# Two unused tiles in the constants pool that move x and xT from 128 to 0 modulo 512 bytes in SBUF

## The chip, the cores and the metric

The kernel runs on one core of one Trainium2 chip. The metric is the device time of one execution in microseconds (us), the median of several runs. The profile comes from one further execution.

## What is computed

One encoder block with float32 weights on 256 tokens of width 1024: a half-step SwiGLU feed-forward, a mixer with two parallel branches, and a second half-step feed-forward. Cut to what matters for the work on the matrix engine:

```python
def block(x):                                     # x: (256, 1024), F = 4096
    h = rmsnorm(x, ffn1_pre_g)
    x = x + 0.5 * rmsnorm((silu(h @ w_gate) * (h @ w_up)) @ w_down, ffn1_post_g)
    h = rmsnorm(x, mix_pre_g)
    q, k, v, f, u, sv, ga, gb = split(h @ w_in)
    o_a = forgetting_attention(q, k, v, f)        # 8 heads of 128, causal, with a decay from f
    o_b = gelu(u) * (w_s @ layernorm(gelu(sv)) + b_s)
    m = sigmoid(ga) * o_a + sigmoid(gb) * o_b
    x = x + rmsnorm(m @ w_out, mix_post_g)
    h = rmsnorm(x, ffn2_pre_g)
    return x + 0.5 * rmsnorm((silu(h @ w_gate2) * (h @ w_up2)) @ w_down2, ffn2_post_g)
```

## The kernel before

**Precision.** Each float32 operand of a large product is split into a high part (rounded to fp32r, the matrix engine's fast float32) and a low part (the remainder): ScalarE casts the high part (L83), VectorE subtracts (L84). A product is three matmuls: high by high, high by low and low by high.

**Tiling.** The normalised activations are transposed on TensorE and kept in `xT` as [128 rows of the width, 8 blocks k, 2 token tiles t, high or low, 128 tokens] (L69, written by `to_xT`, L156 to L162). "Tokens stationary" means that in most products the 128 tokens are the stationary operand, which a weight load (LDWEIGHTS) brings into the array, and 512 columns of a weight matrix are the moving operand. `proj` (L212 to L218) does this for gate, up, v, sv, u, ga, gb and the output projection: for each k it runs `xT[high]` by `hi`, `xT[high]` by `lo`, `xT[low]` by `hi`, so two matmuls of three move `hi` and one `lo`. Every matmul has a weight load of its own, also where two in a row use the same stationary operand.

**Other stationary operands.** The down projection (`down`, L340 to L351) has `hT` as stationary operand, the hidden activations, with the same three terms. Three of the four up blocks of each feed-forward use `fast` (L270 to L329), a Strassen-Winograd scheme with 7 products of 12 matmuls each instead of 8: three of them take their stationary operand from `xT` (tiles `A` twice and `D` once), four from `parts`, sums and differences of quarters of x (tiles `B`, `C` and, the first time, `D`). All of these go through the one matmul call at L285 with the same order of terms.

**Moving xT.** In `attention` (L481) the roles are reversed: `wide` (L191 to L197) has the weights stationary and moves all 512 columns of `xT[:, k]` for the high weights, and the 256 high columns for the low weights. The forget gates (L455) move `xT` as well.

**Memory.** SBUF addresses are given as bytes within a partition; they follow from the order in which the pools and their tiles are made, in steps of 32 bytes. The constants pool comes first, with `x` (L66), `xT` (L69), `ident` (L71), `power` (L72), `idle` (L646) and the small tiles of the mixer. Then come five buffers `raw` of 8192 bytes for loaded weights, four each of `hi` and `lo`, two gains, ten intermediate tiles of 2048 bytes, three buffers of 8192 bytes for `hT` and the mixer's tiles, and `parts`. All rows of `xT`, `hT` and `parts` that one matmul loads are 512 bytes long, and they follow one another at steps of 512 bytes, so each has the same address modulo 512 as its tile.

**Order.** The order on each engine follows from the program and from priorities at build time; all loads go through one queue (SP). The weight buffers are filled some blocks ahead of the products that use them.

Of the kernel before, what the change touches and what calls it, by code (L numbers as in the profile page):

```python
# [15 lines left out]
F32 = mybir.dt.float32  # L16
# [6 lines left out]
P = 128  # L23
# [22 lines left out]
def block(ctx: ExitStack, tc: tile.TileContext, a: dict, out: bass.AP):  # L46
    nc = tc.nc
    const = ctx.enter_context(tc.tile_pool(name="const", bufs=1))
# [14 lines left out]
        return mid.tile(shape, F32, tag="m", name=name)  # L63


    x = const.tile([P, NT, D], F32, name="x")  # L66
    for t in range(NT):
        nc.sync.dma_start(out=x[:, t, :], in_=a["x"][t])
# [1 line left out]

    ident = const.tile([P, P], F32, name="ident")  # L71
    power = const.tile([P, 4], F32, name="power")  # L72
    nc.vector.memset(power, -0.5)

    def gain(name, by=D):
# [689 lines left out]
```

## Time and profile before

| | |
|---|---|
| median of 3 runs | 770.52 us (769.61 to 773.78) |
| profiled execution: its own time | 769.38 us |
| profiled execution: span from first to last instruction | 767.6 us |
| granted TensorE clock, mean over the span | 0.999 |
| TensorE busy, matmuls | 746.9 us, 3446 instructions |
| VectorE busy | 539.0 us, 516 instructions |
| ScalarE busy | 381.0 us, 376 instructions |
| moved by DMA | 141.61 MB, 184 GB/s over the span |

TensorE is read from the chain of work that ended last and from the timeline: a matmul's own recorded duration includes its way through the pipeline, which overlaps with the next matmul, so what it costs is the distance from its start to the next start. In the chain, a run of matmuls is one piece, whose length divided by its count is that distance.

### The profile page before, as it was taken

The numbers are of one execution on the slowest core, as the hardware profiler recorded it, in microseconds if no ns is written. First come the engines' busy times: TensorE is split into PE (matmuls) and PEld (weight loads), VectorE is DVE, ScalarE is ACT, GpSimd is POOL, SyncE is SP. The second block draws the span as 40 slices with busy tenths as digits, with TensorE's granted clock in tenths as the row PEclk, the third lists the DMA queues.
The fourth block names the chain that finished last, engine by engine and source line by source line (L and its number), as shares of the span: only waits on it lengthen the run. The fifth ranks groups of instructions, "written<-read, shape, count | busy, mean of one in ns | idle before, by whom it ended". The sixth has DMA issues, their size and how long they took to land. (4 is left out here: it accounts for less than half of the span.)

```text
span 767.6 us, 8470 instructions
## 1 busy us (share of the span) xinstructions
PE 746.9 (97%) x3446; PEld 608.1 (79%) x3446; DVE 539.0 (70%) x516; ACT 381.0 (50%) x376; POOL 21.5 (3%) x32
## 2 busy tenths in 40 slices
PE   5999999999999999999999999889999999999996
PEld 2888888888888877888888888678888888888885
DVE  6584798589479875746486547858479958947982
ACT  5553465446445474754544435645346545644541
POOL 1000000000000021000020000300000000000000
PEclk9999999999999999999999999999999999999999
DMA  9785158418515835643427435437515741851521
GB/s 338 286 311 191 61 211 293 153 68 338 197 55 213 330 136 184 257 161 110 158 117 275 164 111 219 163 118 266 178 70 198 301 159 59 334 210 55 199 75 56
DMA packets 21974, 141.61 MB, mean 184 GB/s; under 512 B 3184, under 2 KB 3440, under 8 KB 5680
## 3 DMA queue, kind: packets, MB, share of 16 engines
q1 hardware_dynamic: 21936, 141.08, 50.0%
q8 instruction: 27, 0.44, 0.2%
q14 instruction: 11, 0.09, 0.0%
HBM read 140.02 MB, written 1.05 MB: 184 GB/s over the span
## 5 line engine op out<-in xcount | busy, mean ns | idle before, releaser
L217 PE MATMUL g<-hi_g,xT 128*128 128x512 f32 x512 | 166.7, 396 | 0.3 <-ACT hi_g L83 0.2
L350 PE MATMUL y<-hi_d,hT 128*128 128x512 f32 x512 | 148.0, 393 | 0.0
L217 PEld LDWEIGHTS g<-hi_g,xT 128*128 128x128 f32 x512 | 96.4, 188 | 23.1 <-ACT hi_g L83 1.0
L350 PEld LDWEIGHTS y<-hi_d,hT 128*128 128x128 f32 x512 | 95.7, 188 | 20.1
L84 DVE TENSOR_TENSOR lo_g<-raw_g,hi_g 128x2048 fp32r<-128x2048 f32 (+1 forms) x33 | 73.4, 2225 | 44.9 <-ACT hi_g L83 44.9
L217 PE MATMUL g<-lo_g,xT 128*128 128x512 f32 x256 | 101.3, 396 | 2.8 <-DVE lo_g L84 2.7
L84 DVE TENSOR_TENSOR lo_d<-raw_d,hi_d 128x2048 fp32r<-128x2048 f32 x32 | 73.0, 2287 | 39.4 <-ACT hi_d L83 39.4
L350 PE MATMUL y<-lo_d,hT 128*128 128x512 f32 x256 | 81.1, 393 | 0.0
L83 ACT CAST hi_g<-raw_g 128x2048 fp32r<-128x2048 f32 (+1 forms) x33 | 61.2, 1856 | 34.7 <-PE u L217 10.5
L83 ACT CAST hi_d<-raw_d 128x2048 fp32r<-128x2048 f32 x32 | 60.8, 1915 | 26.9 <-PE g L217 8.8
L217 PE MATMUL u<-hi_u,xT 128*128 128x512 f32 x192 | 61.7, 396 | 0.0
L217 PEld LDWEIGHTS g<-lo_g,xT 128*128 128x128 f32 x256 | 48.3, 189 | 14.7 <-DVE lo_g L84 3.8
L350 PEld LDWEIGHTS y<-lo_d,hT 128*128 128x128 f32 x256 | 47.9, 188 | 9.9
L289 DVE TENSOR_TENSOR raw_u<-raw_u,raw_u 128x2048 f32<-128x2048 f32 x24 | 55.0, 2292 | 0.8
L356 ACT ACTIVATE sg<-g 128x512 f32<-128x512 f32 x32 | 18.9, 598 | 67.3 <-PE g L217 67.3
L196 PE MATMUL qk<-xT,hi_qk 128*128 128x512 f32 x128 | 46.3, 400 | 0.0
L83 ACT CAST hi_u_3p<-raw_u 128x2048 fp32r<-128x2048 f32 x14 | 26.6, 1915 | 32.9 <-DVE raw_u L289 25.1
L217 PEld LDWEIGHTS u<-hi_u,xT 128*128 128x128 f32 x192 | 36.1, 188 | 8.3
L84 DVE TENSOR_TENSOR lo_u<-raw_u,hi_u 128x2048 fp32r<-128x2048 f32 x12 | 27.4, 2289 | 16.6 <-ACT hi_u L83 16.5
L84 DVE TENSOR_TENSOR lo_u_3p<-raw_u,hi_u_3p 128x2048 fp32r<-128x2048 f32 x14 | 31.9, 2288 | 9.6 <-ACT hi_u_3p L83 9.6
L217 PE MATMUL u<-lo_u,xT 128*128 128x512 f32 x96 | 37.9, 394 | 0.0
L83 ACT CAST hi_u_1p<-raw_u 128x2048 fp32r<-128x2048 f32 x14 | 26.8, 1914 | 20.3 <-DVE raw_u L289 9.5
(254 smaller groups left out, 1273.2 us busy)
## 6 DMA issues: line engine op xcount, KB each, us to landing
raw_u<-in_u SPq DMA_DIRECT2D x32, 1024.0 KB, 4.8
raw_d<-in_dn SPq DMA_DIRECT2D x32, 1024.0 KB, 4.7
raw_g<-in_g SPq DMA_DIRECT2D x31, 1024.0 KB, 4.9
raw_qk<-in_w_qk SPq DMA_DIRECT2D x8, 1024.0 KB, 5.1
raw_v<-in_w_v SPq DMA_DIRECT2D x4, 1024.0 KB, 5.4
raw_sv<-in_w_sv SPq DMA_DIRECT2D x4, 1024.0 KB, 4.7
raw_u<-in_w_u SPq DMA_DIRECT2D x4, 1024.0 KB, 4.7
raw_ga<-in_w_ga SPq DMA_DIRECT2D x4, 1024.0 KB, 4.7
```

What stands on the lines that cost most here:

```text
L83: return [nc.scalar.copy(out=hi, in_=src), nc.vector.tensor_tensor(out=lo, in0=src, in1=hi.bitcast(F32), op=ALU.subtract)]
L84: nc.vector.tensor_tensor(out=lo, in0=src, in1=hi.bitcast(F32), op=ALU.subtract)]
L196: nc.tensor.matmul(ps, lhsT=hi, rhs=xT[:, k], start=k == 0, stop=False, skip_group_check=True)
L217: nc.tensor.matmul(ps, lhsT=xT[:, kh * 4 + k, t, xs, :], rhs=v, start=kh == 0 and k == 0 and q == 0, stop=kh == 1 and k == 3 and q == 2)
L289: nc.vector.tensor_tensor(out=out, in0=p, in1=q, op=ALU.add)
L350: nc.tensor.matmul(ys[t][c], lhsT=hTs[f // 4][:, f % 4, t, xs, :], rhs=w[:, c * 512:(c + 1) * 512], start=f == 0 and q == 0, stop=f == NF ...
L356: nc.scalar.activation(out=sg, in_=y, func=AF.Silu)
```

## The change

```diff
@@ -63,6 +63,7 @@
         return mid.tile(shape, F32, tag="m", name=name)
 
 
+    const.tile([P, 96], F32, name="pad0")
     x = const.tile([P, NT, D], F32, name="x")
     for t in range(NT):
         nc.sync.dma_start(out=x[:, t, :], in_=a["x"][t])
@@ -70,6 +71,7 @@
 
     ident = const.tile([P, P], F32, name="ident")
     power = const.tile([P, 4], F32, name="power")
+    const.tile([P, 32], F32, name="pad1")
     nc.vector.memset(power, -0.5)
 
     def gain(name, by=D):
```

The two tiles are never written or read. `pad0` takes 384 bytes of each partition, `pad1` 128. The instructions on every engine, their order, their waits, the buffers that each tile gets and the places in PSUM are the same before and after; only addresses in SBUF differ:

| tile | before | modulo 512 | after | modulo 512 |
|---|---|---|---|---|
| `x` | 16512 | 128 | 16896 | 0 |
| `xT` | 24704 | 128 | 25088 | 0 |
| `ident` | 41088 | 128 | 41472 | 0 |
| `power` | 41600 | 128 | 41984 | 0 |
| `idle` | 41632 | 160 | 42144 | 160 |
| `raw`, first buffer | 44288 | 256 | 44800 | 256 |
| `hi`, first buffer | 85248 | 256 | 85760 | 256 |
| `lo`, first buffer | 118016 | 256 | 118528 | 256 |
| `hT`, first buffer | 179456 | 256 | 179968 | 256 |
| `parts` | 204032 | 256 | 204544 | 256 |

Everything from `idle` on moves up by 512 bytes, and so keeps its address modulo 512.

## Rows read from the trace of the kernel before

**Rows 1.** The page: busy time of each engine, granted clock in 40 slices.
```profile
PE 746.9 (97%) x3446; PEld 608.1 (79%) x3446; DVE 539.0 (70%) x516; ACT 381.0 (50%) x376; POOL 21.5 (3%) x32
...
PEclk9999999999999999999999999999999999999999
```

**Rows 2.** Groups by form: line, engine, operation, shapes, count | busy us, mean ns | idle.
```profile
L217 PE MATMUL g<-hi_g,xT 128*128 128x512 f32 x512 | 166.7, 396 | 0.3 <-ACT hi_g L83 0.2
L350 PE MATMUL y<-hi_d,hT 128*128 128x512 f32 x512 | 148.0, 393 | 0.0
...
L217 PEld LDWEIGHTS g<-hi_g,xT 128*128 128x128 f32 x512 | 96.4, 188 | 23.1 <-ACT hi_g L83 1.0
L350 PEld LDWEIGHTS y<-hi_d,hT 128*128 128x128 f32 x512 | 95.7, 188 | 20.1
...
L217 PE MATMUL u<-hi_u,xT 128*128 128x512 f32 x192 | 61.7, 396 | 0.0
...
L217 PE MATMUL v<-hi_v,xT 128*128 128x512 f32 x64 | 20.6, 396 | 0.0
...
L285 PE MATMUL u_1A<-hi_u_1p,xT 128*128 128x512 f32 x32 | 10.7, 395 | 0.0
```

**Rows 3.** The chain that ended last: start us, length us, engine, tile, line, count.
```profile
502.43 16.73 PE g L217 x72
519.16 13.93 PE u L217 x60
...
576.48 2.80 PE u_1A L285 x12
579.28 2.75 PE u_1C L285 x12
582.03 2.72 PE y L350 x12
584.75 2.73 PE u_1B L285 x12
...
738.66 22.74 PE y L350 x100
```

**Rows 4.** Timeline of TensorE in a gate block: start us, length us, what, count.
```profile
505.51 0.64 PE L217 MATMUL g<-hi_g,xT 128*128 128x512 f32 x2
505.99 0.39 PE L217 MATMUL g<-lo_g,xT 128*128 128x512 f32 x1
```

**Rows 5.** Timeline, matmul and the weight load beside it.
```profile
587.31 0.40 PE L285 MATMUL u_1A<-hi_u_1p,xT 128*128 128x512 f32 x1
587.31 0.19 PEld L285 LDWEIGHTS u_1A<-lo_u_1p,xT 128*128 128x128 f32 x1
```

**Rows 6.** Timeline of TensorE in the query and key products, every sixth matmul.
```profile
312.75 0.28 PE L197 MATMUL qk<-xT,lo_qk 128*128 128x256 f32 x1
...
313.80 0.28 PE L197 MATMUL qk<-xT,lo_qk 128*128 128x256 f32 x1
...
314.85 0.28 PE L197 MATMUL qk<-xT,lo_qk 128*128 128x256 f32 x1
```

**Rows 7.** Groups by form: other operations on moved and unmoved tiles.
```profile
L84 DVE TENSOR_TENSOR hT<-hp,hT 128x512 fp32r<-128x512 f32 x32 | 21.4, 684 | 0.0
...
L371 PE MATMUL hp<-ident,sg 128*128 128x128 f32 x128 | 18.5, 272 | 0.0
...
L84 DVE TENSOR_TENSOR xT<-tp_f,xT 128x512 fp32r<-128x512 f32 x8 | 5.2, 684 | 0.0
...
L594 PE MATMUL mx<-vn,ws 128*128 128x128 f32 x32 | 4.2, 274 | 0.0
```

**Rows 8.** DMA issues: what, queue, count, KB each, median us to landing.
```profile
x<-in_x SPq DMA_DIRECT2D x2, 512.0 KB, 3.4
...
out<-x SPq DMA_DIRECT2D x4, 256.0 KB, 2.0
```

## The prediction

> **What bounds the kernel now.** I read three views in this order. First the busy times: the matmuls occupy TensorE for 746.9 of 767.6 us, VectorE is at 70% and ScalarE at 50% [rows 1]. Only 20.7 us of the span lie outside matmuls, so nearly everything the change can do must show as the distance from one matmul to the next, and nothing on another engine can be worth much unless TensorE comes to wait for it. [...]
>
> Second the chain of waits, which gives that distance. With `xT` as stationary operand it is (16.73 + 13.93) / (72 + 60) = 232.3 ns in the gate and up products; with `hT` it is 22.74 / 100 = 227.4 ns in the last long run of the down projection [rows 3]. Third, a control inside one piece of code: the Strassen products of line 285 have the same moving tiles, the same order of terms and the same 12 matmuls, and lie a few us apart. With `xT` stationary (`u_1A`) they take 2.80 / 12 = 233.3 ns each, with `parts` stationary 2.75 / 12 = 229.2 (`u_1C`) and 2.73 / 12 = 227.5 (`u_1B`); a short block with `hT` in between takes 2.72 / 12 = 226.7 [rows 3]. So 5 ns per matmul go with the tile `xT`, not with the line, the loop or the stage.
>
> Where in the matmul the 5 ns lie is not seen directly. The weight loads are recorded with 188 ns for `xT` and for `hT` alike, and the matmuls with 396 against 393 ns [rows 2]. The load for the next matmul begins together with the current one, both at 587.31 us [rows 5], so two reads of SBUF, one of 512 bytes per partition and one of 2048, run side by side in every interval. What sets `xT` apart from `hT`, `parts`, `hi` and `lo` is its address: it begins at 128 modulo 512, all the others at 256, so it alone is not at a multiple of 256. It also lies lowest of all, and the trace before cannot separate the one from the other.
>
> [...]
>
> **The change part by part.** *Instructions.* None is added, removed or moved, and no wait, queue or buffer changes. The padding is never touched. This part costs nothing, and no cover is needed for it.
>
> *xT as stationary operand.* The count: `hi` moves in 512 matmuls for gate, in 192 for up (the mixer's u among them), in 64 for each of v, sv, ga, gb and the output projection, 5 x 64 = 320, and in the Strassen products 32 for each of three `A` and half as many for each of three `D` with `xT`, 96 + 48 [rows 2]. That is 1168; by the order of terms `lo` adds half of it, 584. Together 1752 of the 3446 matmuls. If 0 modulo 512 is as good as 256 modulo 512, each saves 232.3 - 227.4 = 4.9 ns: 1752 x 4.9 = 8.6 us. I take this value because two other tiles, `hT` and `parts`, show it, and because rows of these tiles that begin at 256, 768, 1280 and 1792 modulo 2048 all occur within it; steps of 512 bytes do not matter. Below it the bound is 0 (the address is not the cause). Above it: whether a row at a multiple of 512 is read faster still than one at 256 is not in the trace; I bound it by the same step once more, 17.2 us in all.
>
> *Blocks between.* In the second feed-forward the down projection runs in blocks of 12 between `xT` blocks. The timeline's starts settle after some matmuls behind each change of tile, and the blocks of `parts` vary from 227.5 to 229.2 [rows 3]. If nothing differs in alignment any more, these could all settle at 227.4 or below. The 288 matmuls with `parts` (6 block passes x 4 products x 12) gain between 0 and 1.8 ns, at most 0.5 us. I take 0.3 us.
>
> *xT as moving operand.* In the query and key products, six matmuls (three of 512 columns, three of 256) take 313.80 - 312.75 = 1.05 us, and the next six 314.85 - 313.80 = 1.05 [rows 6]: 350 ns a pair. [...] I take 0.1 us.
>
> *ident, x and power.* The transposes read `ident`, which moves with `xT`. They are recorded with 272 ns, and the mixing product on two tiles that do not change modulo 512 with 274 [rows 7]: no loss to recover, 0. On VectorE the remainder takes 684 ns into `xT` and 684 into `hT` [rows 7]: 0 again. `x` is loaded in 3.4 us, and the output leaves in 2.0 us [rows 8]. These two lie open at the two ends, and only they: in between no transfer touches `x`. Rows cannot price the address there; from 0 to a tenth of 3.4 + 2.0, 0.5 us, I take 0.
>
> [...]
>
> *Does the saving reach the end?* TensorE's waits for the splits in steady work are small (0.3 us before all 512 matmuls of gate [rows 2]) and VectorE has 30% to spare, against a stretch of work that becomes 1.2% shorter. I count the whole saving. If cover runs out somewhere, a weight buffer would be filled late, and it would show as a wait for `lo` or `hi`.
>
> The sum: 8.6 + 0.3 + 0.1 = 9.0 us. The profiled execution took 769.38 us for a span of 767.6, so it would take 760.4; it lies 1.1 us under the median, 770.52, and the median would be 761.5 us.
>
> **The rivals.** *No change.* The cause is the place of `xT` (lowest in memory) or something else about it, and the same 232.3 ns return. The time is 770.5 us. For it: every `xT` row before is both low and misaligned. [...] I give it 0.27.
>
> *Slower: the distance between the two reads counts, not each address.* Moving and stationary rows of the fast group both begin at 256 modulo 512, so they begin in step. `xT` is 128 bytes off that, and will be 256 off. If the two reads collide on a pattern of 512 bytes, half of it may be worse than a quarter. The price: a pair of `xT` matmuls now sometimes takes 505.99 - 505.51 = 0.48 us [rows 4], 240 ns each; if all did, 1752 x (240 - 232.3) = 13.5 us, 784.0 us. It decides as soon as the distance exceeds 232.3 ns, and leaves the band of no change at 232.3 + 3.9 us / 1752 = 234.5 ns. Against it: `hT` rows show no dependence on steps of 512, so only a pattern of exactly 512 would do this, and it may as well help. I give it 0.06.
>
> *Faster than forecast.* An address of 0 modulo 512 is better than 256: up to 17.2 us, 753.3 us. I give it 0.06, most of it for some part of that.
>
> *The change does not do what it says* (the unused tiles get no memory): excluded, since the built program has `x` at 16896 and `xT` at 25088.
>
> **How the numbers follow.** The forecast, 761.5 us, has 0.61; its own range, with 4 to 6 ns per matmul and the small terms at their ends, is 759 to 764. No change has 0.27, slower 0.06, faster than forecast 0.06. To hold 8 in 10 the range must reach the case of no change, whose runs lay from 769.6 to 773.8 us; I take 757 to 772.5. About 0.5%, 3.9 us, is what a measurement can tell from no change. The forecast and the case above it are faster by more: 0.67. No change: 0.27. Slower: 0.06.
>
> **What would show it.** In the profile after, a run of 12 gate matmuls would take 2.73 us in place of 2.79, `u_1A` the same as `u_1B`, and the recorded mean of the `xT` matmuls would fall from 396 ns towards 393 or less. TensorE's busy time would fall by some 9 us to 738, with the other engines' durations unchanged. If the distance stays at 232 ns, the address modulo 512 is not the cause. If it is above, the distance between the two reads is. If it falls but the span does not, there must be new waits for `hi` and `lo`.

## The result and the profile after

The changed kernel takes 762.35 us, the median of five runs, against 772.29 us for the kernel before over six runs, 9.9 us less; the ratio is 0.9869 with a 95% interval of 0.9841 to 0.9898. One run of this kernel at 1920.27 us, one of the kernel with `pad1` alone at 1248.28 us and one of the kernel with `lo` moved at 1064.58 us were slow and are left out of all comparisons. The forecast was 761.5 us. The profiled execution after took 760.05 us for a span of 758.3 us, 9.3 us less than the one before; the sum of the prediction was 9.0.

The busy times, first line of the page of the profile after, against [rows 1]:

```profile
PE 739.0 (97%) x3446; PEld 608.1 (80%) x3446; DVE 538.2 (71%) x516; ACT 381.4 (50%) x376; POOL 21.5 (3%) x32
```

The matmuls lost 7.9 us of busy time. The weight loads, VectorE, ScalarE and GpSimd stand where they were, within 0.8 us. So the whole change lies on TensorE, and there in the matmuls and not in the loads.

The chain of work that ended last, after (start us, length us, engine, tile, line, count; line numbers are two higher than before), against [rows 3]:

```profile
493.96 1.75 PE tp_f L162 x8
495.70 17.38 PE g L219 x72
513.09 13.60 PE u L219 x60
...
569.30 2.72 PE u_1A L287 x12
572.02 2.72 PE u_1C L287 x12
574.74 2.72 PE y L352 x12
577.46 2.72 PE u_1B L287 x12
...
729.36 22.73 PE y L352 x100
```

The 60 up matmuls with `xT` stationary take 13.60 / 60 = 226.7 ns, where 13.93 / 60 = 232.2 stood before. `u_1A` (from `xT`), `u_1B` and `u_1C` (from `parts`) and the short block of `y` (from `hT`) are now alike to 0.01 us, and the long run of the down projection, 22.73 for 22.74, is as it was. One piece went the other way: the 72 gate matmuls take 17.38 us for 16.73. That is the clock, as shown further down.

Groups by form after (line, engine, operation, shapes, count | busy us, mean ns | idle), against [rows 2]:

```profile
L219 PE MATMUL g<-hi_g,xT 128*128 128x512 f32 x512 | 164.7, 393 | 0.5 <-ACT hi_g L85 0.3
L352 PE MATMUL y<-hi_d,hT 128*128 128x512 f32 x512 | 147.4, 392 | 0.0
...
L219 PEld LDWEIGHTS g<-hi_g,xT 128*128 128x128 f32 x512 | 96.8, 189 | 21.1 <-ACT hi_g L85 1.1
...
L287 PE MATMUL u_1A<-hi_u_1p,xT 128*128 128x512 f32 x32 | 10.5, 389 | 0.0
```

The recorded length of the `xT` matmuls falls from 396 to 393 ns and of `u_1A` from 395 to 389; the weight load stays at 188 to 189 ns. No new wait for `hi` appears ahead of the 512 gate matmuls (0.5 us against 0.3).

The query and key products, which move `xT`, in the timeline of TensorE after, at a distance of six matmuls, against [rows 6]:

```profile
312.96 0.28 PE L199 MATMUL qk<-xT,lo_qk 128*128 128x256 f32 x1
...
314.02 0.28 PE L199 MATMUL qk<-xT,lo_qk 128*128 128x256 f32 x1
...
315.08 0.28 PE L199 MATMUL qk<-xT,lo_qk 128*128 128x256 f32 x1
```

Six now take 1.06 us, where it was 1.05. These products gained nothing from the same move, though here too the rows went from 128 bytes apart, modulo 256, to 0.

### The profile page after: what moved, and what is told of

Same layout as the page of the kernel before. It is cut to its first block, busy times and chain, and to the rows that moved or that the text cites. A ratio compares the mean times of both kernels' runs of the same rounds, so it can differ in the third digit from the quotient of the medians.

```text
span 758.3 us, 8470 instructions
## 1 busy us (share of the span) xinstructions
PE 739.0 (97%) x3446; PEld 608.1 (80%) x3446; DVE 538.2 (71%) x516; ACT 381.4 (50%) x376; POOL 21.5 (3%) x32
## 3 DMA queue, kind: packets, MB, share of 16 engines
HBM read 140.02 MB, written 1.05 MB: 186 GB/s over the span
## 5 line engine op out<-in xcount | busy, mean ns | idle before, releaser
L219 PE MATMUL g<-hi_g,xT 128*128 128x512 f32 x512 | 164.7, 393 | 0.5 <-ACT hi_g L85 0.3
```

The costliest lines, as they stand in the source:

```text
L219: nc.tensor.matmul(ps, lhsT=xT[:, kh * 4 + k, t, xs, :], rhs=v, start=kh == 0 and k == 0 and q == 0, stop=kh == 1 and k == 3 and q == 2)
```

## The experiments

Three theories were set against one another. A, the prediction's: an operand costs time where its own row begins off a multiple of 256 bytes. D, taken from the prediction's slower rival: what counts is the distance in bytes, modulo 256, between the row that is moved and the stationary row that is loaded beside it (in nanoseconds, a distance is still that from one matmul's start to the next). P: `xT` is slow because of its place at the lower end of SBUF. All kernels compute the whole block. The diffs are cuts, against the kernel before unless another is named; `...` marks what is left out. In the fences of this section, a row is one of the chain that ended last (start us, length us, engine, tile, line, count), from the kernel that the paragraph is about: `u` x60 stands for the stationary `xT`, `y` x100 for the stationary `hT`, `u_1A` for `xT` and `u_1B` for `parts`.

### One of the two tiles alone

```diff
+    const.tile([P, 96], F32, name="pad0")
     x = const.tile([P, NT, D], F32, name="x")
```

> Only the first of the two tiles: xT at 0 modulo 512, but hi, lo, hT and parts now at 128. Theory A (each operand's own address: a matmul loses some 5 ns if its moving or its stationary row begins off a multiple of 256): every matmul moves a misaligned weight row, so the xT blocks stay near 232 ns and the hT and parts blocks, with both operands misaligned, go to 232 or more; 770 us plus (768 + 288) x 5 ns = 775 us or more. Theory D (only the distance between the two rows modulo 256 counts): xT blocks 232 ns (distance 128), hT and parts blocks 227 (distance 0); 771 us, as before. Theory P (xT is slow because it lies lowest): xT 232, hT 227, 771 us.

```profile
522.03 13.94 PE u L218 x60
...
579.39 2.80 PE u_1A L286 x12
...
741.45 22.73 PE y L351 x100
```

772.28 us, ratio 1.0008 (0.9994 to 1.0022): no change. `xT` is at 0 modulo 512, where the change puts it, and its blocks run at 13.94 / 60 = 232.3 ns. `hT` and the weights it meets are both at 128, and run at 22.73 / 100 = 227.3 ns. The address of each row for itself explains neither.

```diff
     power = const.tile([P, 4], F32, name="power")
+    const.tile([P, 32], F32, name="pad1")
```

> Only the second tile: xT stays at 128 modulo 512, hi, lo, hT and parts move to 384, so that all of them begin off a multiple of 256, but at distances of 0 modulo 256 from one another. Theory A: all blocks at 232 ns or more, 775 us or more. Theory D: all blocks at 227 ns, 762 us, as fast as with both tiles. Theory P: xT 232, hT 227, 771 us.

```profile
515.12 13.60 PE u L218 x60
...
571.34 2.72 PE u_1A L286 x12
...
731.34 22.73 PE y L351 x100
```

762.06 us, ratio 0.9881 (0.9846 to 0.9916). Here `xT` has not moved at all, every large buffer begins off a multiple of 256, and the kernel is as fast as with the whole change: 226.7 ns. A falls with this run, and P too, since `xT` lies where it always lay. D had both right.

### The other position at distance 0, and the other place

```diff
+    const.tile([P, 32], F32, name="pad0")
     x = const.tile([P, NT, D], F32, name="x")
...
     power = const.tile([P, 4], F32, name="power")
+    const.tile([P, 96], F32, name="pad1")
```

> x and xT at 256 modulo 512, the same as the weights, everything behind where the change puts it. Theories A and D: 227 ns in all stationary-xT blocks, 762 us, so 512 is not needed and 256 does; the query and key products, which move xT, would show whether 0 or 256 suits them (353 ns a pair after the change, 350 before). If 0 modulo 512 mattered as such: slower than 762. Theory P: 232 ns, 771 us.

```profile
515.37 13.61 PE u L219 x60
```

Here `x` and `xT` begin at 256 modulo 512, as `hi` and `lo` do. The 60 up matmuls take 13.61 us, 226.8 ns, and the kernel 761.49 us, ratio 0.9873 (0.9854 to 0.9892). Between `xT` at 0 and at 256 modulo 512, with the weights at 256 both times, there is no difference: 256 bytes make no distance, and 512 is not needed. The query and key products, which the expectation also names, stay at 1.06 us for six.

```diff
+    high = ctx.enter_context(tc.tile_pool(name="high", bufs=1))
...
-    xT = const.tile([P, KT, NT, 2, P], F32R, name="xT")
+    high.tile([P, 88], F32, name="pad2")
+    xT = high.tile([P, KT, NT, 2, P], F32R, name="xT")
```

> xT alone in a pool of its own at the upper end of SBUF (212608, 128 modulo 512), all other large buffers 16384 bytes lower at unchanged addresses modulo 512, x as before. Theories A and D: xT blocks at 232 ns, hT and parts 227, 771 us as before. Theory P: xT blocks at 227 ns, 762 us, and perhaps the tile that now lies lowest (raw, which TensorE does not read) without effect.

```profile
521.54 13.95 PE u L219 x60
...
578.88 2.80 PE u_1A L287 x12
...
740.98 22.74 PE y L352 x100
```

771.63 us, ratio 1.0002 (0.9985 to 1.0019). With `xT` at the other end of SBUF, in a pool behind all others, and the distance kept at 128, nothing changes. P has fallen a second time.

### Other distances

Four kernels put `x` and `xT` 32, 64, 192 and 224 bytes beyond the weights, modulo 256; only the sizes of the two unused tiles differ (`pad0` 40, 48, 80 and 88 float32 columns, `pad1` 88, 80, 48 and 40), which together always take 512 bytes. The first of them:

```diff
+    const.tile([P, 40], F32, name="pad0")
     x = const.tile([P, NT, D], F32, name="x")
...
     power = const.tile([P, 4], F32, name="power")
+    const.tile([P, 88], F32, name="pad1")
```

> x and xT at 288 modulo 512, hi, lo, hT and parts at 256: the stationary xT row begins 32 bytes beyond the moving row, modulo 256. If every distance other than 0 costs what 128 costs: xT blocks at 232 ns, 771 us. If the cost grows with the distance: between 227 and 232 ns, 762 to 767 us. [...] hT and parts blocks 227 ns in each case.

> As the run at 32 bytes, with xT 64 bytes beyond the moving row modulo 256. Every distance alike: 232 ns, 771 us. Growing with the distance: about 229 to 230 ns, 766 us. [...]

> xT 192 bytes beyond the moving row, which is 64 before it modulo 256. Every distance alike: 232 ns, 771 us. If the cost depends on how far apart they are, whichever is ahead: the same as at 64. If it depends on which is ahead: different from 64.

> xT 224 bytes beyond the moving row, 32 before it modulo 256. Every distance alike: 232 ns, 771 us. Whichever is ahead: the same as at 32. Which is ahead counts: different from 32.

```profile
521.93 13.99 PE u L219 x60
...
741.22 22.71 PE y L352 x100
```

These two rows are of the kernel at 32 bytes, the next of the one at 64, then two of the one at 192 and one of the one at 224.

```profile
522.63 14.00 PE u L219 x60
```

```profile
518.37 13.73 PE u L219 x60
...
735.56 22.73 PE y L352 x100
```

```profile
523.35 14.00 PE u L219 x60
```

With the earlier runs the distances are these (the third column is the length of the piece of 60 up matmuls, divided by 60):

| distance of `xT` from the weights, modulo 256 | kernel | ns a matmul | ratio to before (95%) |
|---|---|---|---|
| 0 | the change | 226.7 | 0.9869 (0.9841 to 0.9898) |
| 0 | only `pad1` | 226.7 | 0.9881 (0.9846 to 0.9916) |
| 0 | `xT` at 256 | 226.8 | 0.9873 (0.9854 to 0.9892) |
| 32 | `pad0` of 40 | 233.2 | 1.0004 (0.9989 to 1.0020) |
| 64 | `pad0` of 48 | 233.3 | 1.0012 (0.9993 to 1.0031) |
| 128 | before | 232.2 | 1 |
| 128 | only `pad0` | 232.3 | 1.0008 (0.9994 to 1.0022) |
| 128 | `xT` high | 232.5 | 1.0002 (0.9985 to 1.0019) |
| 192 | `pad0` of 80 | 228.8 | 0.9934 (0.9895 to 0.9973) |
| 224 | `pad0` of 88 | 233.3 | 1.0009 (0.9994 to 1.0024) |

The cost does not grow with the distance: 32 bytes cost as much as 64 or 128. It is not the same for both sides either, for 192 (64 behind) costs 2.1 ns and 64 ahead costs 6.6, while 32 and 224 agree. No tried distance beats 0. A simple rule for what lies between was not found.

### The same distance for other tiles

```diff
+    gap = ctx.enter_context(tc.tile_pool(name="gap", bufs=1))
+    gap.tile([P, 32], F32, name="pad2")
     big = ctx.enter_context(tc.tile_pool(name="big", bufs=3))
```

> The changed kernel with one more unused tile of 128 bytes ahead of the buffers of hT and of parts: these begin at 384 modulo 512, hi and lo at 256, xT at 0. If the distance between the moving and the stationary row counts, for whatever tile: xT blocks stay at 227 ns, the long run of the down projection goes from 227.3 to 232 ns a matmul and the parts blocks from 2.72 to 2.79 us; (768 + 288) x 5 ns = 5 us more than the change, 767 us. If something about xT was the cause: 762 us and no slower block.

```profile
519.11 13.61 PE u L221 x60
...
575.75 2.76 PE u_1A L289 x12
...
584.09 2.79 PE u_1B L289 x12
...
738.05 23.34 PE y L354 x100
```

769.51 us, ratio to before 0.9966 (0.9952 to 0.9981). Built on the changed kernel, this one makes `hT` and `parts` what `xT` was: the long run of the down projection goes from 22.73 to 23.34 us, 233.4 ns a matmul, and `u_1B` from 2.72 to 2.79, while the `xT` blocks stay fast. So the effect belongs to the distance and not to the tile. The time is 2.5 us above the expectation of 767. About 1.2 of it is the size of the cost, 233.4 - 227.3 = 6.1 ns where 5 were expected, over 1056 matmuls. Another part is in `u_1A`, 2.76 where 2.72 was expected: a block with the right distance pays too when it comes behind one with the wrong distance.

### One moving tile of three at the wrong distance

```diff
     wts = ctx.enter_context(tc.tile_pool(name="wts", bufs=4))
+    gap = ctx.enter_context(tc.tile_pool(name="gap", bufs=1))
+    gap.tile([P, 32], F32, name="pad2")
+    low = ctx.enter_context(tc.tile_pool(name="low", bufs=4))
+    gap2 = ctx.enter_context(tc.tile_pool(name="gap2", bufs=1))
+    gap2.tile([P, 32], F32, name="pad3")
...
-        lo = wts.tile([P, 2048], F32R, tag="lo", name=f"lo_{name}")
+        lo = low.tile([P, 2048], F32R, tag="lo", name=f"lo_{name}")
```

> Built on the kernel with the second tile alone (all rows at 0 from one another modulo 256, 762 us), with the four lo buffers in a pool of their own 128 bytes off: only the matmuls that move lo, one of three, run beside a weight load at a distance of 128. If the cost arises between a moving row and the weight load that runs at the same time: the intervals that move lo lengthen by some 5 ns and the others do not, 936 x 5 ns = 4.7 us, 767 us. If a slip, once made, carries over into the next matmuls, the hi intervals lengthen too, up to the 232 ns of the kernel before, 771 us.

The diff is against the kernel with `pad1` alone. The chain:

```profile
520.42 14.00 PE u L223 x60
...
578.00 2.78 PE u_1A L291 x12
...
740.55 23.14 PE y L356 x100
```

A stretch of the 60 up matmuls in the timeline of TensorE (start us, length us, what, count):

```profile
521.19 0.40 PE L223 MATMUL u<-lo_u,xT 128*128 128x512 f32 x1
521.43 0.63 PE L223 MATMUL u<-hi_u,xT 128*128 128x512 f32 x2
521.89 0.40 PE L223 MATMUL u<-lo_u,xT 128*128 128x512 f32 x1
```

772.54 us, ratio 1.0007 (0.9992 to 1.0022): the whole gain is gone, though only one matmul of three moves a row at the wrong distance. If the 20 of 60 that move `lo` had alone lost 5.5 ns, the piece would have taken 13.60 + 0.11 = 13.71 us; it took 14.00. Nor do the 20 bear the whole loss: in the trace's nanoseconds the starts repeat at distances of 236 (behind a first `hi`), 234 (behind `lo`) and 230 (behind a second `hi`), where the kernels with all rows in step repeat 227, 227 and 226. So the cost is not paid by the matmul at the wrong distance alone, as the second of the two expectations had it.

That the time equals that of the kernel before is a coincidence. Here `hT` and `parts` meet the moved `lo` too, so that 2808 matmuls share the loss, and not the 1752 of `xT`. It is smaller elsewhere than in the up products: 23.14 - 22.73 = 0.41 us over the run of 100, 4.1 ns each. At 5 ns for each of them the time would have been some 14 us above the 762 us, and not 10.

### The clock behind a pause

In the profile after, matmuls behind the pause of TensorE at the start of the second feed-forward lie 0.43 us apart. Timeline of TensorE after (start us, length us, what, count), and the busy times of two stretches, first after and then before (in each: us; busy us and count for PE, PEld, DVE, ACT, POOL; granted clock; DMA share; GB/s):

```profile
495.36 0.77 PE L219 MATMUL g<-hi_g,xT 128*128 128x512 f32 x1
495.93 0.63 PE L219 MATMUL g<-lo_g,xT 128*128 128x512 f32 x1
496.36 1.05 PE L219 MATMUL g<-hi_g,xT 128*128 128x512 f32 x2
497.21 0.63 PE L219 MATMUL g<-lo_g,xT 128*128 128x512 f32 x1
```

```profile
495.00:498.00 3.00, 3.00 (x11) 2.47 (x10) 2.92 (x6) 0.87 (x2) 0.00 (x0) 0.53 0.55 227
```

```profile
497.00:505.00 8.00, 4.67 (x24) 3.52 (x23) 7.15 (x10) 4.12 (x8) 1.93 (x2) 1.00 0.81 305
```

After, the granted clock is 0.53 of full over these 3 us; before, it was full (1.00) over the 8 us that hold the same pause. Two kernels fill the pause with 12 matmuls on the idle tile, one built on the changed kernel and one on the kernel before:

```diff
+FILL = {("f2", 1, 0): 12}
...
         ps = bank(f"tp_{name}{t}{c}")
+        for _ in range(FILL.get((name, t, c), 0)):
+            nc.tensor.matmul(ps, lhsT=idle[:, 0:P], rhs=idle, start=True, stop=True)
```

> The changed kernel with 12 matmuls on the idle tile in the pause of TensorE ahead of the second transposes of the second feed-forward (3.9 us from the last gate matmul to the first transpose). In the profile after, the granted clock is 0.53 of full from 495 to 498 us, behind that pause, and matmuls lie 427 ns apart. If the fall of the clock follows from the pause: no such stretch, clock 0.999, 1 to 3 us less than the changed kernel, 760 us. If not: the same time or 0.1 us more.

> The kernel before with the same 12 matmuls in the same pause. If its own scatter (769 to 774 us) comes from that clock: 769 us with clock 0.999 and a ratio to the kernel before of 0.997. The distance between this and the run with the fill on the changed kernel is then the gain of the two tiles alone, 9 us by the sum.

The filled pause in the timeline of TensorE, the chain behind it, and the stretch in the columns of above, all of the changed kernel with the fill:

```profile
491.26 2.76 PE L163 MATMUL tp_f<-idle 128*128 128x512 bf16 x12
494.82 1.38 PE L165 MATMUL tp_f<-ident,hn_f 128*128 128x128 f32 x8 [0.79 <-DVE hn_f L171]
495.96 0.48 PE L222 MATMUL g<-hi_g,xT 128*128 128x512 f32 x1
```

```profile
496.20 16.36 PE g L222 x72
512.56 13.60 PE u L222 x60
```

```profile
480.00:500.00 20.00, 17.95 (x86) 13.14 (x85) 17.08 (x20) 10.87 (x15) 5.46 (x6) 1.00 0.66 237
```

The clock stays full there (1.00), and the 72 gate matmuls take 16.36 us, 1.02 less than in the profile after. Of the other profiles without the fill only that of the kernel before has a full clock behind this pause; in the ten others it is 0.66 to 0.68 over the 5 us from the last transposes on, and their 72 gate matmuls take 17.65 to 18.34 us, for 16.73 there. Both profiles with the fill have it full (1.00 over the 20 us around the pause), so that the fill is the likely cause, from two profiles. The mean over the whole span, 0.996 and 0.995, is not the 0.999 expected: in the page of the kernel before with the fill, the first of the 40 slices (19.2 us) stands at 8 tenths and all others at 9; on the page of the changed kernel with the fill all stand at 9, which does not show where the rest of its clock went. On the kernel before, the fill gives 769.84 us, ratio 0.9978 (0.9967 to 0.9990), a small gain whose interval excludes 1. On the changed kernel it gives 759.9 us, ratio to before 0.9854 (0.9838 to 0.9871), the fastest kernel of this study; but against the change alone, 0.9869 (0.9841 to 0.9898), the intervals overlap, so that its own share there is seen in the trace and not in the time. With the fill on both sides the two tiles are worth 769.84 - 759.9 = 9.9 us.

## Why the prediction was right, point by point

**What bounds the kernel.** Right. The gain came from the distance between matmuls, TensorE remained the bound, and in steady work the cover held: the wait for `hi` is 0.5 us for 0.3. Two pauses of TensorE at the start of the second feed-forward did grow, from 0.95 to 1.15 and from 3.30 to 3.50 us.

**The cause.** The number was right and the stated cause was not. The prediction observed that `xT` alone began off a multiple of 256, and took the address of each row as the cause. It is the distance, modulo 256 bytes, between the moving and the stationary row. Before the change the two descriptions pick out the same tile, since everything else lay at 256; they part only where all lies off 256 together (`pad1` alone, fast) or where the weights do (`pad0` alone, slow). The distance was in the prediction, as the mechanism of its slower rival, with 0.06. What was wrong there was the size of the pattern: for 512 bytes, the change would have brought half a pattern; for 256 it brought 0. The remark in that rival that `hT` depends on no step of 512 excluded patterns longer than 512, and `x256` then excluded 512 itself. So the forecast came out by luck in this respect: the change happened to set right both the addresses that the prediction went by and the distance that counts. (The 0.48 us in that rival's price is a difference of two rounded starts; in the trace's nanoseconds that pair takes 474, 237 each, and the 784.0 us are some 5 too high.)

**xT as stationary operand.** 8.6 us from 1752 x 4.9 ns. The count stands; the difference was mis-sized. The up blocks went from 232.2 to 226.7, 5.5 ns, so 1752 x 5.5 = 9.6 us. The 227.4 taken for the fast side came from the run of 100, which stayed at 227.3, since its first dozen starts, behind transposes, lie 224 to 323 ns apart before they settle at 227; the short block at 2.72 / 12 = 226.7 [rows 3] was the better measure.

**Blocks between.** 0.3 us was taken for `parts` and nothing for `hT`. The direction was right: `u_1C` went from 2.75 to 2.72. How large such an after-effect can be is seen in the kernel with `hT` and `parts` off, where `u_1A`, itself at distance 0, took 2.76 us behind a block of `hT`: half of its gain was lost. In the second feed-forward from the start of the 60 up matmuls to that of the run of 100, before 738.66 - 519.16 = 219.50 us and after 729.36 - 513.09 = 216.27: 3.23 us less. This stretch has 492 `xT` matmuls, of 588 in the feed-forward (384 gate, 96 up, 108 Strassen) less the 96 of the first gate block, worth 492 x 5.5 = 2.7 us; the other 0.5 us are the blocks between, and that for one feed-forward of two. Summed from start to start in the two traces, 0.4 of it lies at `hT` and 0.2 at `parts`: the 0.3 for `parts` over both was the right size, and the term at nothing, `hT`, was the larger one.

**xT as moving operand.** 0.1 us was taken, a term that no run shows: six of these matmuls took 1.06 us in the profile after, for 1.05 before, so the gain was none. These products went from a distance of 128 to 0 as well, so the rule of the distance, too, would have had them gain; it is shown for the products with tokens stationary, and not here. Why is open.

**ident, x and power.** Right at 0, as far as can be told: `x` was loaded in 3.3 us for 3.4, the output left in 2.0 for 2.0. Over all profiles the load takes 3.1 to 3.3 us where `x` begins at a multiple of 256 and 3.2 to 3.4 elsewhere, too close to tell them apart. The first gate matmul began at 11.21 us in the profile after and at 12.19 before; in the other kernels that start came at any time up to 14.06 us, whatever the address of `x`, so 1 us of the profiled difference is not the change's.

**What the sum did not have.** The half clock behind the pause. From the first of the eight transposes to the first up matmul the profile after takes 513.09 - 493.96 = 19.13 us, and the one with the fill 512.56 - 494.82 = 17.74: 1.4 us, in the profile after and in none of the stages of the profile before. Of the profiled 9.3 us, then, 9.6 and about 1 for the blocks between come from the distance, 1.0 from the earlier start, and 1.4 was lost to the clock, with some 0.4 in two pauses that were longer; that leaves 9.8, within 0.5 us of what was measured. That the 9.0 of the sum lies so near the 9.3 is in part luck: the two mis-sized terms and the earlier start add 2.7 us to it, and the clock and the pauses take 1.8 away.

**The rival of no change**, with 0.27, rested on the place of `xT`; two runs exclude it. With nothing altered but the distance between the moving and the loaded row, a matmul takes 226.7 ns (at 0) or 233.3 (at 64). That it is the two reads that hinder each other is the nearest explanation and is not shown, since no trace here records a read.

## What to carry to other kernels

Where float32 matmuls of 512 columns follow one another with a weight load each, as in the products with tokens stationary here, look at the start of the moving row and of the stationary row modulo 256 bytes, and let all of them agree; here this was worth 1.2% for 128 bytes of padding, with `pad1` alone. Compare the time from one matmul's start to the next across tiles that go through the same line of code: a constant 5 ns between two tiles was the whole case, and no view of waits shows it. A cause read from one layout should be tried in a second one that separates it from its nearest neighbour, since here the right number stood on the wrong one of two.

## What the hardware showed that was not expected

With a weight load for each matmul, the starts fall into a repeating pattern, and the address of one row against the other decides which: 227, 227 and 226 ns with all rows in step, and 236, 234 and 230 in the up products with one moving row of three at the wrong distance. Distances of 32, 64, 128 and 224 bytes cost alike (5.5 to 6.6 ns), 192 about a third of that, and none of those tried is below 0. Where the period of 256 bytes comes from was not tried, and neither was whether the stationary row of the same matmul counts or that of the next, which is loaded meanwhile: in these kernels both begin at the same address modulo 256 but at the edges of blocks. A pause of TensorE of the same place and nearly the same length was followed by the half clock in the profile after (0.53 over 3 us) and by the full one in the profile before (1.00 over 8 us), so the pause alone did not decide it; in both profiles with 12 idle matmuls in it the clock stayed at 1.00.
